# The swapped copy of q: from a VectorE copy to an integer operation in layer 1, and into the DMA transpose in layer 2

## The chip, the core and the metric

The kernel runs on one core of a Trainium2 chip. The number that counts is the device time of one execution in microseconds. The kernel before took 1673.78 us in the median of three runs (1671.57 to 1674.27).

## What is computed

Two layers work on a residual stream of 1024 positions and 1024 channels, each `x <- x + W_out(mixer(RMSNorm(x)) * silu(gate))`, with 16 heads of 64. Layer 1 is causal attention with a forgetting bias, layer 2 is windowed attention in three dilation groups whose results are weighted by their softmax sums.

```python
def fox_mixer(h, w_in, b_f, q_g, k_g):                 # layer 1
    q, k = rms_norm(q, q_g), rms_norm(k, k_g)          # per head, over 64 channels
    c = cumsum(log_sigmoid(f_logit))
    s = einsum('bqhd,bkhd->bhqk', q, k) * scale + c_q - c_k ; causal mask ; softmax ; @ v
def dsw_mixer(h, cos, sin, w_in, q_g, k_g):            # layer 2
    q, k = partial_rotary(rms_norm(q, q_g)), partial_rotary(rms_norm(k, k_g))
    for g, (window, dilation) in enumerate(((128, 1), (512, 4), (2048, 16))):
        o_g, lse_g = dilated_window_attention(q[g], k[g], v[g], window, dilation)
    o = sum_g softmax_g(lse_g) * o_g
```

The inputs and the result are float32.

## The kernel before

**Two halves for each number.** TensorE multiplies float16. To keep float32's precision each operand is split into a high and a low float16 half, and a product is made of three matmuls (high by high, high by low, low by high). The projections (`project`, L688, matmul on L693) stream `xh` and `xl`, each against a slab of weights: 24 matmuls of 384 columns per tile of 128 positions. The columns are those of two heads at once: keys, queries and values.

**From a projection to q and k.** Two tiles of positions make a pair. `heads_tile` (L786) multiplies keys and queries by the gains into `u` (VectorE, L788) and squares them on ScalarE (L793). `heads_sums` sums the squares on VectorE (L806, L808). `heads_pair` (L810) applies the rotation in layer 2 on GpSimd (L820 to L823: `ra`, `rb`, `u`), makes the inverse root (ScalarE L826 to L828, VectorE L829, L830), multiplies `u` by it (VectorE L832), and splits `u` into `hl`: the high half on ScalarE (L834), the low half on GpSimd (L835). `hl` is `[128, 2, 4, 2, 64]`: position, tile of the pair, two keys and two queries, high and low, channel.

**The turn.** `turn` (L837) sends `hl` through one DMA transpose (L840, issued from SyncE's queue SP) of 8 blocks of 128 by 128. In each block of the result `qk_t` the partitions 0 to 63 hold the 64 channels' high half and 64 to 127 the low half of one key or query. A matmul of a query block with a key block contracts over all 128 partitions and gives high by high plus low by low. The two mixed products need the query with its halves exchanged. Before, `qs` holds this: two VectorE copies (L843), each of 64 partitions and 512 float16, move the upper half of the query blocks down and the lower half up. They wait for the transpose to land.

**Scores.** `scores` (L858) takes for each head two matmuls (L863): the first with the query out of `qk_t`, the second with `qs`. The rows of scores go through VectorE (L1110 in layer 1, L1335 in layer 2: bias or mask and the maximum), ScalarE (exponent L1337 or L906, high half of `ph` L1347 or L909), GpSimd (low half L1348 or L912), a second DMA transpose (`ptt<-ph`, L1349 or L913), and the matmuls with the values (L920 to L922). In layer 2 there are 24 rounds of weights with 4 pairs each, 96 pairs; in layer 1 there are 8 rounds, 32 pairs. The scores of a pair are asked for 16 ticks after it (`lsd`), where one tick is two of the eight slabs of a projection.

**What sets the order.** The program is written in one line of time (`Flow`), and `order_engines` (L426) then fixes every engine's order. `plan_engines` (L323) walks through all instructions with a table of durations (`Step.lasts`, L206), of those VectorE operations that keep GpSimd out and are kept out by it (`Step.locks`, L191), and of latest starts worked out from the order on TensorE (`latest_starts`, L304). A copy between two SBUF tiles is such a locking operation in the table, with 60 + 0.45 ns for each column; an operation with a scalar is not, with 110 + 1.04 ns for each. Each engine and the SP queue carry out their instructions in that order, and one that waits holds up all behind it. GpSimd's low half of `ph`, the low half of `hl` and the rotation share one such order. The pools around the change: two buffers of `hl`, six of `qk_t` and `qs` in layer 1, three of each in layer 2.

Of the kernel before, what the change touches and what calls it, by code (L numbers as in the profile page):

```python
# [22 lines left out]
P = 128  # L23
# [5 lines left out]
HD = 64  # L29
# [407 lines left out]
def trunk(ctx, tc, ins, out, cfg):  # L437
    nc = tc.nc
# [7 lines left out]
    def pool(name, bufs, space=None):  # L446
        kw = {} if space is None else dict(space=space)
        return book.pool(ctx.enter_context(tc.tile_pool(name=name, bufs=bufs, **kw)), name, bufs, space)
# [3 lines left out]
    sb = pool("sb", 2)  # L452
# [16 lines left out]
    def lay(shape, dtype, name, tag):  # L469
        return layer["pool"].tile(shape, dtype, name=name, tag=tag, bufs=layer["bufs"][tag])  # L470
# [339 lines left out]
    def heads_pair(gi, t, hd):  # L810

        u, sq, w = hd
        if gi > 0:
            half = ROT // 2
            ti = (gi - 1) * NT + t
            c = cs[:, ti : ti + 2].unsqueeze(2)
            s = sn[:, ti : ti + 2].unsqueeze(2)
            ra = sm.tile([P, 2, 4, ROT], F32, name="ra", tag="ra", bufs=2)
            rb = sm.tile([P, 2, 4, ROT], F32, name="rb", tag="rb", bufs=2)
            nc.gpsimd.tensor_mul(ra, u[:, :, :, :ROT], c.broadcast_to([P, 2, 4, ROT]))  # L820
            nc.gpsimd.tensor_mul(rb[:, :, :, :half], u[:, :, :, half:ROT], s[:, :, :, :half].broadcast_to([P, 2, 4, half]))
            nc.gpsimd.tensor_mul(rb[:, :, :, half:], u[:, :, :, :half], s[:, :, :, half:].broadcast_to([P, 2, 4, half]))
            nc.gpsimd.tensor_add(u[:, :, :, :ROT], ra, rb)  # L823
        v, a, y = w["v"], w["a"], w["y"]
        r = sm.tile([P, 2, 4], F32, name="rs_y", tag="rs_y4")
        nc.scalar.activation(r, v, AF.Ln)  # L826
        nc.scalar.activation(r, r, AF.Exp, scale=-0.5)
        nc.scalar.activation(a, r, AF.Square)  # L828
        nc.vector.scalar_tensor_tensor(a, a, -0.5, v, ALU.mult, ALU.mult)  # L829
        nc.vector.scalar_tensor_tensor(y, a, 1.5, r, ALU.add, ALU.mult)  # L830
        hl = sb.tile([P, 2, 4, 2, HD], F16, name="hl", tag="hl", bufs=cfg["hb"])
        nc.vector.tensor_mul(u, u, y.unsqueeze(3).broadcast_to([P, 2, 4, HD]))  # L832

        nc.scalar.copy(hl[:, :, :, 0], u)  # L834
        nc.gpsimd.tensor_sub(hl[:, :, :, 1], u, hl[:, :, :, 0])  # L835

        def turn():  # L837
            qk_t = lay([P, 8, P], F16, name="qk_t", tag="qk_t")
            qs = lay([P, 2, 2, P], F16, name="qs", tag="qs")
            nc.sync.dma_start_transpose(qk_t, hl.rearrange("p i a b d -> p (i a b d)"))  # L840
            qk = qk_t.rearrange("p (i a) s -> p i a s", i=2)
            for a in (0, HD):
                nc.vector.tensor_copy(qs[a : a + HD], qk[HD - a : P - a, :, 2:4])  # L843
            return qk, qs

        return turn
# [26 lines left out]
    def v_tile(w):  # L873
        vt = lay([P, NT, 2, 129], F16, name="vt", tag="vt")
        nc.scalar.activation(vt[:, :, :, 128], w.sw.unsqueeze(2).broadcast_to([P, NT, 2]), AF.Copy, scale=lim[:, w.layer, 3:4])
        return vt
# [125 lines left out]
    with book.early(nc, cfg["rush"]):  # L1002
        gain_scale(0, gt)
        nb = column_factor(0)
        gain_xt(0)
        split_xt(0, nb)
    with book.early(nc, cfg["rush"] / 2):
        nb = column_factor(1)
# [173 lines left out]
    for hp in range(NHP):  # L1182
# [11 lines left out]
        vt = v_tile(w)  # L1194
        for t in range(NT):
            ps = project(w, tile_cols(0, t))
# [12 lines left out]
            if hp == NHP - 1:  # L1209

                a = max(flow.now + 1, s0 + cfg["due"][t] - 4 * NT + cfg["lpf"] + 9)
# [219 lines left out]
    for ci, (hp, g) in enumerate(order):  # L1431
# [5 lines left out]
        vt = v_tile(w)  # L1437
        qks = [None]
        for t in range(NT):
            if ci == NHP - 1:  # L1440
                reload_x(t)
            ps = project(w, tile_cols(g, nth_tile(g, t)))
# [21 lines left out]
            else:  # L1464
                cmb = {}
# [28 lines left out]
    layer["cm"].__exit__(None, None, None)  # L1494


CFG = dict(out={(False, 0): (), (True, 0): ((18, 20, 22, 24), (0, 0, 1, 1), 3, (4, 6, 8, 10)), (True, 1): ((18, 20, 22, 24), (14, 15, 17, 18), 24, (33, 35, 37, 39))}, take=(((33, 34, 37, 40), 42), ((62, 63, 66, 69), 71)), rush=2000, gate=(((6, 7, 8, 9), (0, 0, 1, 1), 4, (5, 6, 7, 9)), ((44, 45, 46, 47), (26, 28, 30, 32), 36, (38, 40, 42, 44)), ()), bc=((1, 0, 26), (1, 1, 28), (0, 0, 38), (0, 1, 46)), wpool=3, rbufs=8, most=(0, 2), lcm=7, ps=0, pv=100, ph_=100, ph=1, wbufs=8, pl=3, um=3, lpf=8, lsd=((16, 16), (16, 14), (14, 11)), ty2=((0, 4), (1, 5)), hb=2, ub=2, qb=1, nb=3, fox=(((0, 0, 2, 2), (2, 4)), ((0, 0), (4, 4))), due=(29, 33, 39, 45, 35, 41, 49, 57), l1=dict(ga=7, ptt=4, ph=3, p=4, qk_t=6, qs=6, vt=3, gsl=3), l2=dict(ga=4, cmb=4, gsd=4, ptt=3, ph=3, p=2, qk_t=3, qs=3, og=3, vt=3, gsl=3, par=1), wload=(18, 20, 22, 24), wbound=(0, 1, 3, 4), wscale=8, wsplit=(10, 16, 22, 12))


def host_layout(inputs):  # L1500
# [49 lines left out]
```

## Time and profile before

| | |
|---|---|
| three timed runs | 1674.27, 1671.57, 1673.78 us |
| profiled execution | 1674.25 us, its span 1672.1 us |
| granted TensorE clock, mean | 0.996 |
| layer 1's attention | 140 to 560 us of the span |
| layer 2's attention | 620 to 1600 us |
| output projection of layer 2 | from 1600 us |

A group's row names the line, the engine, the operation, what it writes and reads, how often it ran, its busy time, the mean duration in ns, and how long the engine stood idle before it and for what. PE is the matmul part of TensorE, PEld its weight load, DVE is VectorE, ACT ScalarE, POOL GpSimd, SPq the queue that issues the DMAs. A wait's row says who waited for whom, for how long in all, how many times, and the longest. TensorE's busy time counts overlapping matmuls once, and a matmul of 384 columns is shown with 324 ns although the next one begins 163 ns later (192 of them take 31.24 us in the chain of waits); a stall shorter than that overlap doesn't appear as idle.

### The profile page before, as it was taken

Reading aid. Unit: us, or ns where it says so; the run is one execution under the profiler, and the core shown is the slowest. Engines: PE = TensorE matmul, PEld = TensorE weight load, DVE = VectorE, ACT = ScalarE, POOL = GpSimd, SP = SyncE. Lnnn points to the kernel's source line nnn. Section 1 sums busy time; section 2 is a strip of 40 time slices with the busy share of each in tenths; the row PEclk is TensorE's granted clock in tenths of the full one; section 3 lists DMA queues with packets and bytes.
Section 4 is the critical chain, followed back from the end, with each engine's and each line's share of the span. In section 5 each row is a group of like instructions: output and inputs, shape, how many; then the busy total and the mean of one; then the engine's idle time right before and its main releaser. Section 6 shows DMA issues by size and latency. Waiting matters only on the chain.

```text
span 1672.1 us, 37759 instructions
## 1 busy us (share of the span) xinstructions
PE 1615.3 (97%) x13342; PEld 1045.3 (63%) x13342; DVE 1271.4 (76%) x3791; ACT 1067.4 (64%) x2746; POOL 893.2 (53%) x1049
## 2 busy tenths in 40 slices
PE   5999999999989999999999999999999999999999
PEld 3666776766765456666666666666666666666544
DVE  7857888878876597577777797878787888878851
ACT  6656777777766477566666677656665666656630
POOL 4303656666645242155555566667576775857430
PEclk9999999999999999999999999999999999999999
DMA  6344999999999785246665785767657576666852
GB/s 239 114 133 116 204 208 199 211 174 195 213 201 234 218 255 177 88 116 151 144 140 127 164 198 131 174 134 167 134 148 147 129 189 134 150 146 153 191 160 98
DMA packets 597326, 276.07 MB, mean 165 GB/s; under 512 B 444672, under 2 KB 561408, under 8 KB 597136
## 3 DMA queue, kind: packets, MB, share of 16 engines
q1 hardware_dynamic: 597136, 273.67, 69.5%
q8 instruction: 104, 1.70, 0.4%
q14 instruction: 86, 0.70, 0.1%
HBM read 124.35 MB, written 41.22 MB: 99 GB/s over the span
## 4 chain that ended last, share of the span: by engine, by line
PE 56%; DVE 16%; DMA 10%; issue 6%; POOL 5%; ACT 4%; SPq 2%; POOLq 0%; DVEq 0%; ACTq 0%
PE pj L693 41%; PE pj L718 7%; PE s L863 4%; DMA qk_t<-hl 3%; DVE qs L843 3%; DVE w L659 3%; DMA ptt<-ph 2%; DMA raw<-in_w_dsw 1%; POOL ph L1348 1%; POOL hl L835 1%; DVE vm L632 1%; DVE p L1110 1%; DMA yt<-y_d 1%; ACT p L906 1%; DVE u L788 1%
## 5 line engine op out<-in xcount | busy, mean ns | idle before, releaser
L693 PE MATMUL pj<-w,xh 128*128 128x384 f16 (+2 forms) x4864 | 1173.3, 324 | 12.3 <-ACT w L658 4.8
L693 PE MATMUL pj<-w,xl 128*128 128x384 f16 (+2 forms) x2432 | 787.3, 324 | 3.6 <-DVE xl L1265 3.5
L693 PEld LDWEIGHTS <-xh 128*128 128x128 f16 x4864 | 467.9, 98 | 285.8 <-issue 9.3
L693 PEld LDWEIGHTS <-xl 128*128 128x128 f16 x2432 | 238.2, 98 | 159.0 <-issue 5.6
L912 POOL TENSOR_TENSOR ph<-p,ph 128x512 f16<-128x512 f32 (+3 forms) x176 | 172.7, 1001 | 141.2 <-issue 78.8
L1348 POOL TENSOR_TENSOR ph<-p,ph 128x768 f16<-128x768 f32 (+2 forms) x96 | 156.8, 1633 | 112.4 <-ACT ph L1347 100.1
L835 POOL TENSOR_TENSOR hl<-u,hl 128x512 f16<-128x512 f32 x128 | 156.9, 1226 | 82.6 <-ACT hl L834 81.5
L843 DVE COPY qs<-qk_t 64x512 f16<-64x512 f16 x256 | 152.7, 597 | 24.9 <-DMA qk_t<-hl 18.7
L718 PE MATMUL pj<-xh,w 128*128 128x512 f16 x512 | 158.1, 382 | 6.9 <-DVE xr L1487 3.0
L793 ACT ACTIVATE sq<-pj 128x256 f32<-128x256 f32 x256 | 95.7, 377 | 90.4 <-DVE u L788 88.2
L863 PE MATMUL s<-qk_t 128*128 128x128 f16 (+1 forms) x752 | 144.4, 246 | 3.1 <-DMA qk_t<-hl 1.5
L863 PE MATMUL s<-qk_t,qs 128*128 128x128 f16 (+1 forms) x752 | 141.4, 247 | 5.6 <-DVE qs L843 5.2
L659 DVE SCALAR_TENSOR_TENSOR w<-raw,sws,w 128x768 f16<-128x768 f32 x96 | 135.7, 1420 | 4.4 <-ACT w L658 4.3
L788 DVE TENSOR_TENSOR u<-pj,gr 128x256 f32<-128x256 f32 x256 | 106.4, 418 | 36.7 <-PE pj L693 34.8
L906 ACT ACTIVATE p<-p,acc 128x512 f32<-128x512 f32 (+2 forms) x192 | 109.4, 607 | 36.7 <-DVE acc L1110 36.4
L718 PEld LDWEIGHTS <-w 128*128 128x128 f16 x768 | 74.5, 98 | 90.7 <-issue 9.8
L1337 ACT ACTIVATE p<-p,og 128x128 f32<-128x128 f32 (+1 forms) x256 | 104.9, 443 | 28.2 <-DVE og L1335 27.3
L920 PEld LDWEIGHTS <-ptt 128*128 128x128 f16 x1136 | 105.9, 98 | 19.0 <-DMA ptt<-ph 7.6
L630 ACT ACTIVATE jk<-raw 128x768 f16<-128x768 f32 (+2 forms) x88 | 72.2, 820 | 64.2 <-DMA raw<-in_w_dsw 36.6
L834 ACT CAST hl<-u 128x512 f16<-128x512 f32 x128 | 78.8, 616 | 52.4 <-DVE u L832 42.6
L921 PEld LDWEIGHTS <-ptt 128*128 128x128 f16 x1136 | 105.2, 96 | 11.2
L1335 DVE CUSTOM_DVE_ANT_0 p<-s,band 128x256 f32<-128x256 f32 (+1 forms) x256 | 89.7, 373 | 29.0 <-PE s L863 28.8
(212 smaller groups left out, 3003.3 us busy)
## 6 DMA issues: line engine op xcount, KB each, us to landing
raw<-in_w_dsw SPq DMA_DIRECT2D x96, 384.0 KB, 3.9
raw<-in_w_fox SPq DMA_DIRECT2D x32, 384.0 KB, 4.1
og_d<-og SPq DMA_DIRECT2D x64, 132.0 KB, 2.4
cmb<-og_d SPq DMA_DIRECT2D x64, 132.0 KB, 2.7
bc<-c_d SPq DMA_DIRECT2D x32, 256.0 KB, 4.1
gs_d<-ge SPq DMA_DIRECT2D x32, 192.0 KB, 2.1
xt<-in_xt SPq DMA_DIRECT2D x16, 256.0 KB, 5.0
gsf<-gs_d SPq DMA_DIRECT2D x64, 64.0 KB, 2.4
```

What stands on the lines that cost most here:

```text
L659: nc.vector.scalar_tensor_tensor(w[:, 1, :, :n], raw, self.sw, w[:, 0, :, :n], ALU.mult, ALU.subtract)
L693: nc.tensor.matmul(ps[:, :n], a[:, k, cols], w.slab(k, j), start=(k == 0 and i == 0), stop=(k == KT - 1 and i == 2))
L718: nc.tensor.matmul(ps[m], ws[h].slab(k, j)[:, m * P : (m + 1) * P], a[:, k, 512 * b : 512 * (b + 1)], start=(k == 0 and x == 0), stop=(k = ...
L788: nc.vector.tensor_mul(u[:, t % 2].rearrange("p (a b) d -> p a b d", a=2), ps[:, : 4 * HD].rearrange("p (a b d) -> p a b d", a=2, b=2), gr ...
L835: nc.gpsimd.tensor_sub(hl[:, :, :, 1], u, hl[:, :, :, 0])
L843: nc.vector.tensor_copy(qs[a : a + HD], qk[HD - a : P - a, :, 2:4])
L863: nc.tensor.matmul(s[:, c0 : c0 + cnt * P].rearrange("p (c s) -> p c s", c=cnt), q, kk[:, j : j + cnt, e], start=(h == 0), stop=(h == 1 an ...
L906: nc.scalar.activation(p, p, AF.Exp, bias=acc, scale=-1.0)
L912: (nc.gpsimd if pool_l else nc.vector).tensor_sub(ph[:, e, 1, cols], p, ph[:, e, 0, cols])
L920: nc.tensor.matmul(o[:, e, :], hi, vt[:, j, e, HD:], start=(b == 0), stop=False, skip_group_check=True)
L921: nc.tensor.matmul(o[:, e, :HD], hi, vt[:, j, e, :HD], start=False, stop=False, skip_group_check=True)
L1348: nc.gpsimd.tensor_sub(ph[:, 1], st["p"], ph[:, 0])
```

## The change

In layer 1 (`gi` is 0) the two operations that make `qs` stay in their place, after the transpose. Their views are read as 32-bit integers, 256 columns in place of 512, and the copy becomes a bitwise OR with zero.

In layer 2 `qs` is gone. `hl` has 6 rows in place of 4 for each tile: a VectorE copy writes the queries a second time, with high and low exchanged, after GpSimd has made the low half. The transpose then has 12 blocks in place of 8, and the swapped query is `qk[:, :, 4:]`. So the copy is one of 128 partitions and 512 float16 for each pair in place of two of 64 partitions, and stands ahead of the transpose, not behind it.

```diff
-        hl = sb.tile([P, 2, 4, 2, HD], F16, name="hl", tag="hl", bufs=cfg["hb"])
+        nb = 6 if gi else 4
+        hl = sb.tile([P, 2, nb, 2, HD], F16, name="hl", tag="hl", bufs=cfg["hb"])
         nc.vector.tensor_mul(u, u, y.unsqueeze(3).broadcast_to([P, 2, 4, HD]))
 
-        nc.scalar.copy(hl[:, :, :, 0], u)
-        nc.gpsimd.tensor_sub(hl[:, :, :, 1], u, hl[:, :, :, 0])
+        nc.scalar.copy(hl[:, :, :4, 0], u)
+        nc.gpsimd.tensor_sub(hl[:, :, :4, 1], u, hl[:, :, :4, 0])
+        if gi:
+            nc.vector.tensor_copy(hl[:, :, 4:], hl[:, :, 2:4, ::-1])
 
         def turn():
-            qk_t = lay([P, 8, P], F16, name="qk_t", tag="qk_t")
-            qs = lay([P, 2, 2, P], F16, name="qs", tag="qs")
+            qk_t = lay([P, 2 * nb, P], F16, name="qk_t", tag="qk_t")
             nc.sync.dma_start_transpose(qk_t, hl.rearrange("p i a b d -> p (i a b d)"))
             qk = qk_t.rearrange("p (i a) s -> p i a s", i=2)
+            if gi:
+                return qk, qk[:, :, 4:]
+            qs = lay([P, 2, 2, P], F16, name="qs", tag="qs")
             for a in (0, HD):
-                nc.vector.tensor_copy(qs[a : a + HD], qk[HD - a : P - a, :, 2:4])
+                dst, src = (v.bitcast(I32) for v in (qs[a : a + HD], qk[HD - a : P - a, :, 2:4]))
+                nc.vector.tensor_single_scalar(dst, src, 0, ALU.bitwise_or)
             return qk, qs
```

The table of buffers loses `qs=3` in layer 2. Since the planner takes durations and locks by kind of operation, the order on every engine is made anew. On TensorE it is nearly the same. The two places below belong to the 63rd pair of layer 2, in the profile before at 1278 to 1290 us.

VectorE before, from the inverse root of the next pair to the sum of outputs; `qs<-qk_t` are the two copies, `vt` the values' low half, `u<-pj` the first product of the next tile:

```order
L829 SCALAR_TENSOR_TENSOR pj<-pj,rs_v 128x8
L830 SCALAR_TENSOR_TENSOR pj<-pj,rs_y 128x8
L788 TENSOR_TENSOR u<-pj,gr 128x256
L832 TENSOR_TENSOR u<-u,pj 128x512
L843 COPY qs<-qk_t 64x512
L799 SCALAR_TENSOR_TENSOR vt<-pj,vt 128x2x64
L843 COPY qs<-qk_t 64x512
L1387 TENSOR_TENSOR ob<-ob,cmb 128x260
```

VectorE in the change, the 63rd pair's own second product of `u` and the copy into `hl`:

```order
L830 SCALAR_TENSOR_TENSOR pj<-pj,rs_y 128x8
L1375 TENSOR_REDUCE mm<-cmb 128x4
L833 TENSOR_TENSOR u<-u,pj 128x512
L788 TENSOR_TENSOR u<-pj,gr 128x256
L838 COPY hl<-hl 128x2x256
L799 SCALAR_TENSOR_TENSOR vt<-pj,vt 128x2x64
```

The copy now stands two rows behind the product from which ScalarE and GpSimd still have to make `hl`, and the next tile's work stands behind it.

GpSimd before, at the same pair (`ph` is a low half of the exponents, `hl` that of keys and queries, `ra` and `rb` the rotation of the next pair, `cmb` the weighting of the groups):

```order
L1376 TENSOR_TENSOR wt<-mm,cmb 128x8
L1348 TENSOR_TENSOR ph<-p,ph 128x768
L835 TENSOR_TENSOR hl<-u,hl 128x8x64
L820 TENSOR_TENSOR ra<-u,cs 128x128
L821 TENSOR_TENSOR rb<-u,sn 128x8x8
```

GpSimd in the change:

```order
L1382 TENSOR_TENSOR wt<-mm,cmb 128x8
L836 TENSOR_TENSOR hl<-u,hl 128x2x4x64
L1354 TENSOR_TENSOR ph<-p,ph 128x768
L1385 TENSOR_TENSOR cmb<-cmb,wt 128x8x65
L820 TENSOR_TENSOR ra<-u,cs 128x128
```

Here `hl` has moved ahead of `ph`, so that a long GpSimd operation follows it at once; elsewhere in layer 2 mostly `ra` follows, as before.

More of the change, by code (lines that the diff above doesn't have):

```diff
@@ L1494, in trunk @@
     layer["cm"].__exit__(None, None, None)
-CFG = dict(out={(False, 0): (), (True, 0): ((18, 20, 22, 24), (0, 0, 1, 1), 3, (4, 6, 8, 10)), (True, 1): ((18, 20, 22, 24), (14, 15, 17, 18), 24, (33, 35, 37, 39))}, take=(((33, 34, 37, 40), 42), ((62, 63, 66, 69), 71)), rush=2000, gate=(((6, 7, 8, 9), (0, 0, 1, 1), 4, (5, 6, 7, 9)), ((44, 45, 46, 47), (26, 28, 30, 32), 36, (38, 40, 42, 44)), ()), bc=((1, 0, 26), (1, 1, 28), (0, 0, 38), (0, 1, 46)), wpool=3, rbufs=8, most=(0, 2), lcm=7, ps=0, pv=100, ph_=100, ph=1, wbufs=8, pl=3, um=3, lpf=8, lsd=((16, 16), (16, 14), (14, 11)), ty2=((0, 4), (1, 5)), hb=2, ub=2, qb=1, nb=3, fox=(((0, 0, 2, 2), (2, 4)), ((0, 0), (4, 4))), due=(29, 33, 39, 45, 35, 41, 49, 57), l1=dict(ga=7, ptt=4, ph=3, p=4, qk_t=6, qs=6, vt=3, gsl=3), l2=dict(ga=4, cmb=4, gsd=4, ptt=3, ph=3, p=2, qk_t=3, qs=3, og=3, vt=3, gsl=3, par=1), wload=(18, 20, 22, 24), wbound=(0, 1, 3, 4), wscale=8, wsplit=(10, 16, 22, 12))
+CFG = dict(out={(False, 0): (), (True, 0): ((18, 20, 22, 24), (0, 0, 1, 1), 3, (4, 6, 8, 10)), (True, 1): ((18, 20, 22, 24), (14, 15, 17, 18), 24, (33, 35, 37, 39))}, take=(((33, 34, 37, 40), 42), ((62, 63, 66, 69), 71)), rush=2000, gate=(((6, 7, 8, 9), (0, 0, 1, 1), 4, (5, 6, 7, 9)), ((44, 45, 46, 47), (26, 28, 30, 32), 36, (38, 40, 42, 44)), ()), bc=((1, 0, 26), (1, 1, 28), (0, 0, 38), (0, 1, 46)), wpool=3, rbufs=8, most=(0, 2), lcm=7, ps=0, pv=100, ph_=100, ph=1, wbufs=8, pl=3, um=3, lpf=8, lsd=((16, 16), (16, 14), (14, 11)), ty2=((0, 4), (1, 5)), hb=2, ub=2, qb=1, nb=3, fox=(((0, 0, 2, 2), (2, 4)), ((0, 0), (4, 4))), due=(29, 33, 39, 45, 35, 41, 49, 57), l1=dict(ga=7, ptt=4, ph=3, p=4, qk_t=6, qs=6, vt=3, gsl=3), l2=dict(ga=4, cmb=4, gsd=4, ptt=3, ph=3, p=2, qk_t=3, og=3, vt=3, gsl=3, par=1), wload=(18, 20, 22, 24), wbound=(0, 1, 3, 4), wscale=8, wsplit=(10, 16, 22, 12))
 def host_layout(inputs):
```

## The prediction

> **What bounds the kernel now.** I read the busy shares first, then a table by stage, then who waited for whom on TensorE. The page's first part and the chain of waits by line:
>
> ```profile
> PE 1615.3 (97%) x13342; PEld 1045.3 (63%) x13342; DVE 1271.4 (76%) x3791; ACT 1067.4 (64%) x2746; POOL 893.2 (53%) x1049
> PE pj L693 41%; PE pj L718 7%; PE s L863 4%; DMA qk_t<-hl 3%; DVE qs L843 3%; DVE w L659 3%; DMA ptt<-ph 2%; DMA raw<-in_w_dsw 1%; POOL ph L1348 1%; POOL hl L835 1%; DVE vm L632 1%; DVE p L1110 1%; DMA yt<-y_d 1%; ACT p L906 1%; DVE u L788 1%
> ```
>
> TensorE works for 97% of the span. The chain gives 3% to the copies on L843, 50 us, but that is no gain to be had: a chain runs through buffers and orders while TensorE keeps working beside it. What the change can return is TensorE's idle time where it waits for q.
>
> The attention of layer 1 and of layer 2 as two stretches (TensorE, weight load, VectorE, ScalarE, GpSimd, clock, DMA share), then the instructions that touch `qs` alone (TensorE, weight load, VectorE):
>
> ```profile
> 140.00:560.00 420.00, 404.69 (x4156) 280.95 (x4155) 324.56 (x1035) 306.56 (x738) 236.49 (x230) 0.99 0.94 201
> 620.00:1600.00 980.00, 966.11 (x7812) 626.80 (x7811) 778.82 (x2359) 633.63 (x1749) 590.67 (x761) 1.00 0.65 150
> ...
> 140.00:560.00 420.00, 71.14 (x320) 31.28 (x320) 36.32 (x64) 0.99 0.94 201
> 620.00:1600.00 980.00, 70.26 (x432) 40.89 (x432) 116.39 (x192) 1.00 0.65 150
> ```
>
> In layer 2 TensorE idles 980 - 966.1 = 13.9 us. VectorE is at 79% there, 15% of that in the copies. Waits of TensorE and of its weight load, layer 2 ahead of the second line of dots, layer 1 behind it (total, times, longest):
>
> ```profile
> PE s L863 <- DVE qs L843: 4.0, 5, 1.6
> PE s L863 <- DMA qk_t<-hl: 1.5, 3, 0.9
> PE pj L693 <- DVE peak L897: 1.2, 3, 0.8
> PE pj L693 <- DVE u L832: 0.8, 4, 0.2
> PE pj L693 <- DVE vt L799: 0.7, 2, 0.4
> ...
> PEld L863 <- DVE qs L843: 6.3, 9, 1.8
> PEld L863 <- DMA qk_t<-hl: 2.4, 4, 1.0
> ...
> PE s L863 <- DVE qs L843: 1.2, 2, 0.9
> PEld L863 <- DVE qs L843: 2.5, 3, 1.3
> ```
>
> For q, layer 2 loses between 4.0 + 1.5 = 5.5 us (idle matmul part) and 6.3 + 2.4 = 8.7 us (idle weight load, which also sees waits that the end of the last matmul covers). I take 7, in 9 + 4 = 13 waits. Layer 1 loses 1.2 to 2.5.
>
> **One late pair, step by step.** The 63rd pair of layer 2, the rows of each engine in turn:
>
> ```profile
> 1280.24 1.16 POOL L835 TENSOR_TENSOR hl<-u,hl 128x512 f16<-128x512 f32 x1
> 1281.36 0.46 POOL L820 TENSOR_TENSOR ra<-u,cs 128x128 f32<-128x128 f32 x1
> ...
> 1286.44 1.16 POOL L835 TENSOR_TENSOR hl<-u,hl 128x512 f16<-128x512 f32 x1
> ...
> 1282.17 1.24 SPq L840 DMA_TRANSPOSE qk_t<-hl  x1
> ...
> 1286.72 1.02 DVE L843 COPY qs<-qk_t 64x512 f16<-64x512 f16 x1 [2.11 <-DMA qk_t<-hl]
> 1287.76 0.29 DVE L799 SCALAR_TENSOR_TENSOR vt<-pj,vt 128x128 f16<-128x128 f32 x1
> 1288.06 0.74 DVE L843 COPY qs<-qk_t 64x512 f16<-64x512 f16 x1
> ...
> 1286.75 0.34 PE L863 MATMUL s<-qk_t 128*128 128x128 f16 x2 [0.27 <-DMA qk_t<-hl]
> 1288.86 0.23 PE L863 MATMUL s<-qk_t,qs 128*128 128x128 f16 x1 [1.57 <-DVE qs L843]
> ```
>
> GpSimd ends `hl` at 1281.40, the transpose is issued at 1282.17 and lands near 1286.7. The first score matmul starts; the second needs both copies, which end at 1288.80. They take 1.02 and 0.74 us, and the first overlaps GpSimd's operation from 1286.44 to 1287.60. So the copies are 2.1 us of the way behind the landing, and TensorE idles 0.27 + 1.57.
>
> **Prices.** The copy's durations (min, median, max in ns) in layer 2 and in layer 1, and operations of its kind: integers with a constant, float32 with a constant, and two inputs, most of 128 or 192 columns:
>
> ```profile
> L843 DVE COPY qs<-qk_t x192: 285/290/2198, 717.1 to 1590.5; 64x512 f16<-64x512 f16 x192
> ...
> L843 DVE COPY qs<-qk_t x64: 286/394/1278, 140.5 to 511.9; 64x512 f16<-64x512 f16 x64
> ...
> L1297 DVE TENSOR_SCALAR par_i<-par_i x1: 217/217/217, 645.7 to 645.7; 128x128 int32<-128x128 int32 x1
> ...
> L1046 DVE TENSOR_SCALAR zt<-zt x1: 220/220/220, 87.8 to 87.8; 128x128 f32<-128x128 f32 x1
> L1047 DVE TENSOR_TENSOR zt<-zt,fa x1: 279/279/279, 88.3 to 88.3; 128x128 f32<-128x128 f32 x1
> ...
> L545 DVE TENSOR_SCALAR rt<-rt_pf x8: 177/183/1268, 564.4 to 566.1; 128x24 f32<-128x24 f32 x8
> L555 DVE TENSOR_SCALAR rt<-rt x5: 252/260/261, 567.3 to 576.1; 128x192 f32<-128x192 f32 x5
> L557 DVE TENSOR_TENSOR rt<-rt x5: 357/358/359, 568.0 to 576.7; 128x192 f32<-128x192 f32 x5
> ```
>
> Undisturbed, a copy takes 285 ns; its mean in layer 2 is 116.39 / 192 = 606 ns, so 0.32 us of holding on average, up to 1.9.
>
> *Layer 1's integer operation.* With a constant, 128 columns take 217 to 220 ns and 192 take 260, so (260 - 220) / 64 = 0.63 ns a column, and 256 columns come to 260 + 64 x 0.63 = 300 ns. On the slower line of two inputs, (358 - 279) / 64 = 1.23, they come to 437. The one integer row lies on the fast line, so I take 300, the copy's own time. Whether GpSimd still holds it up no row shows; float32 with a constant meets a hold (1268 against a median of 183 on L545), and being as fast, I take it that integers do. Layer 1 then changes by 0 us, with bounds of -2.5 (its waits for `qs` gone) and +2.5 (as many again).
>
> *Layer 2's removal and addition.* 192 copies of 606 ns go; 96 copies of 512 columns come, at 0.29 us plus the holding. For the holding I have two rows: the 0.32 us of today's copies, and GpSimd's mean operation of 590.67 / 761 = 0.78 us at a load of 590.67 / 980 = 60%, hence 0.47 if the copy, woken by GpSimd's own end of `hl`, finds the next one started and waits it out. I take 0.4, so a copy of 0.7 us. It lies on the way to the scores, between `hl` and the transpose.
>
> *The longer transpose.* The same queue already sends 8 and 12 blocks for the probabilities: three of 512 columns from 1096 us, four of 768 from 1062 us. Issue in ns, then landing in us:
>
> ```profile
> L1349 SPq DMA_TRANSPOSE ptt<-ph x3: 1232/1232/1232, 1096.3 to 1112.7; - x3
> DMA to landing us min/median/max: 2.7/2.7/4.3
> ...
> L1349 SPq DMA_TRANSPOSE ptt<-ph x4: 1401/1420/2235, 1062.9 to 1089.6; - x4
> DMA to landing us min/median/max: 3.2/3.4/4.0
> ```
>
> The undisturbed landing grows from 2.7 to 3.2, 0.5 us for each of 96 transposes. That is 48 us more of the 16 DMA engines in 980, the share going from 0.65 to about 0.70. The issue takes 0.19 us more of SP, 18 us in all, hidden unless SP has fallen behind.
>
> **The sum.** On the way of a late pair go two copies and what stands between and ahead of them: 2 x 0.606 = 1.21 us by the mean, 2.1 in the pair above. There come 0.7 + 0.5 = 1.2. So a late pair gains between 0 and 0.9 us. With 0.4 for each of the 13 waits, of which many are shorter than that, I count 3 of the 7 us as gone: **-3.0** (bounds -7 and, where the copy meets a long `ph` on GpSimd, +8, below). VectorE's load in layer 2 falls by 116.4 - 96 x 0.7 = 49 us, from 79% to 74%; TensorE's other waits for VectorE there (`peak`, `u`, `vt` and four smaller) are about 5 us, of which I take a fifth: **-1.0** (bounds -5 and 0). Busier DMA engines and SP: **+0.5** (0 to +2). Layer 1: **0**. In all -3.5. Against the profiled execution's 1674.25 us (a span of 1672.1 and 2.15 around it) that is 1670.75; it lies 0.47 above the median of the runs shown, so the median goes from 1673.8 to **1670.3**. The cover under all of this is TensorE's own work: a pair's scores come some 16 us behind its projection, and 83 of 96 pairs don't make it wait today. If every pair became 1 us later than I think, only those 13 and a few beside them would show it.
>
> **Rivals.**
>
> *A late copy (slower).* The copy wakes when GpSimd ends `hl`, and GpSimd's next instruction is ready at that instant, as `ra` 1281.36 behind `hl` above. Where the new order puts `ph` there, it holds the copy for a whole long operation:
>
> ```profile
> L1348 POOL TENSOR_TENSOR ph<-p,ph 128x768 f16<-128x768 f32 x40 | 66.3, 1658 | 56.6 <-ACT ph L1347 56.6
> ```
>
> Then the copy takes 0.29 + 1.66 = 1.95, and the way changes by 1.95 + 0.5 - 1.21 = +1.2 us. SP stands at the transpose meanwhile, with the next loads and the probabilities' transposes behind it. The row orders have `ph` behind `hl` in 14 of 96 pairs; if those delays reach half of the 13 waits, that is +8, less the 1 from a freer VectorE: **1681**. It decides when the added holding is over 0.9 us at the late pairs. For it: the maximum of 2198 ns. Against: GpSimd mostly goes on with `ra`, 0.46 us. [...]
>
> *Nearly all waits go.* The freer VectorE makes `u` and the maxima earlier, so late pairs aren't late: -7 and -2 beside it, **1665**. For it: the pair above was late because its copies met other work. Against: the landing took 4.5 us there, which VectorE doesn't change.
>
> *The integer operation is free of GpSimd.* It would take 300 ns in place of a mean 36.32 / 64 = 567, 17 us of VectorE in layer 1, and end its 2.5 us of waits: 1670.3 - 2.5 = **1668**. Against: TensorE idles little for it. [...]
>
> *The change does nothing.* Landing and copy give back what the copies took: **1673.8**.
>
> **How the numbers follow.** About 0.2%, 3.3 us, is what this kernel's runs can tell from no change. The forecast of -3.5 has 0.48 and lies on that line: 0.25 faster, 0.23 same. Nearly all waits go: 0.14, faster. The free integer operation: 0.06 (0.04 faster, 0.02 same). Nothing: 0.10, same. The late copy: 0.22 (0.21 slower, 0.01 same). That makes 0.43 faster, 0.36 same, 0.21 slower. The forecast's own range is 1667 to 1674. The whole range, 1663 to 1681, takes in the bounds on the good side and half of the late copy; less than 2 in 10 lie outside.
>
> **What would show it.** Right: L838 with 96 copies of about 0.7 us and VectorE near 74% in layer 2; transposes of 12 blocks landing in 3.2 us or more; TensorE's waits for `qk_t` in layer 2 near 4 us with none for `qs`; L849 near 300 ns at best, with a median and a maximum as before. Wrong: a minimum under 250 ns on L849 or a maximum under 400; copies of 1.5 us; waits for `qk_t` over 9 us; idle time of TensorE in layer 2 above 14 us; or a gain or loss in the stretch from 430 to 620 us, of which I have said nothing and which the new order also touches.

## The result and the profile after

The changed kernel takes 1663.99 us (median of four runs, 1662.55 to 1665.39) beside 1674.03 us (1671.57 to 1677.13) for the kernel before on the same chip: a ratio of 0.9945, 95% interval 0.9929 to 0.9961. That is 10 us less by the medians and 9 by the ratio. The forecast was 1670.3, in a range of 1663 to 1681 that holds the time, by 1 us at its lower end; the forecast's own range of 1667 to 1674 does not. The sign is right, but the gain is nearly three times the 3.5 us forecast and lands on the price given for the rival "nearly all waits go" (1665). The profiled execution took 1665.39 us with a span of 1663.6, against 1674.25 and 1672.1 before.

Where in the program the time went is read from the rows of the transposes of layer 2, whose first and last start stand behind the durations (min, median, max in ns). Before:

```profile
L840 SPq DMA_TRANSPOSE qk_t<-hl x96: 1231/1240/4789, 713.9 to 1584.6; - x96
```

After, with the time from issue to landing:

```profile
L842 SPq DMA_TRANSPOSE qk_t<-hl x96: 1384/1461/4393, 713.7 to 1577.3; - x96
DMA to landing us min/median/max: 3.2/3.7/7.1
```

The first transpose starts 0.2 us earlier and the last 7.3 us earlier. So in these two profiled executions nothing was gained in layer 1 and up to 714 us; about 7.1 of the 8.5 us of the span were gained over the 96 pairs of layer 2, and the last 1.2 behind them.

The busy shares of the engines on the profile's page after:

```profile
PE 1612.1 (97%) x13342; PEld 1045.5 (63%) x13342; DVE 1198.8 (72%) x3695; ACT 1063.0 (64%) x2746; POOL 893.5 (54%) x1049
```

The chain of waits after can be followed back only to 439 us (the shares on its page add up to 73%), so the chains of the two pages don't compare as a whole. Both cover 620 to 1600 us: there TensorE's projections (L693) are 50.0% of the stretch before and 72.8% after, and the 3.7% of the copies on L843 are gone. The two stretches of the attention in the kernel after, layer 1 and layer 2 (TensorE, weight load, VectorE, ScalarE, GpSimd, clock, DMA share):

```profile
140.00:560.00 420.00, 405.38 (x4168) 282.12 (x4167) 326.89 (x1033) 306.09 (x737) 241.23 (x230) 1.00 0.93 201
620.00:1600.00 980.00, 971.00 (x7864) 629.88 (x7862) 704.58 (x2267) 630.74 (x1751) 587.02 (x761) 1.00 0.71 165
```

TensorE idles 980 - 971.0 = 9.0 us in layer 2, against 13.9. That is 4.9 us of a gain of some 7. Over the whole span the idle time fell by 5.3 of 8.5 us, and the other 3.2 are busy time, 1615.3 to 1612.1 for the same 13342 matmuls. Those may be stalls shorter than the 0.16 us by which two matmuls overlap (324 ns shown, the next one after 163), which count as busy; no row shows them one by one. VectorE's load in the stretch fell by 74 us, from 778.8 to 704.6, where 49 were forecast; 72 of these are the copies. Layer 1 is as it was (404.7 busy and 405.4). Who waited for whom in layer 2 of the kernel after (total, times, longest): TensorE, behind the first dots its weight load, behind the second VectorE:

```profile
PE s L869 <- DMA qk_t<-hl: 4.2, 4, 1.5
PE pj L693 <- DVE xl L1271: 1.0, 1, 1.0
PE pj L718 <- DVE xr L1493: 1.0, 1, 1.0
PE pj L693 <- DVE peak L903: 0.9, 2, 0.7
PE pj L693 <- DVE u L833: 0.9, 6, 0.2
...
PEld L869 <- DMA qk_t<-hl: 6.4, 6, 1.9
...
DVE hl L838 <- POOL hl L836: 49.8, 38, 2.3
```

The scores no longer wait for `qs`, but they wait longer for the landing: 4.2 us in place of 5.5 for both, and 6.4 in place of 8.7 at the weight load. By these rows the scores' waits shrank by 1.3 to 2.3 us, far less than the time did. VectorE stands idle for `hl` ahead of the new copies for 49.8 us in 38 waits, more than the 44.2 us that they take.

The durations (min, median, max in ns) of the copy of layer 2:

```profile
L838 DVE COPY hl<-hl x96: 280/295/1726, 713.3 to 1577.0; 128x512 f16<-128x512 f16 x96
```

And of the integer operation of layer 1:

```profile
L849 DVE TENSOR_SCALAR qs<-qk_t x64: 286/346/1274, 140.0 to 511.9; 64x256 int32<-64x256 int32 x64
```

The integer operation takes 286 ns undisturbed, as the copy of 512 float16 columns did (286), and its maximum stays (1274 beside 1278). 33 of the 64 take over 330 ns, and in the trace each of these overlaps a GpSimd operation that began ahead of it; the longest, at 388.62 us, ends 0.15 us behind the `ph` beside it. So GpSimd holds it up like the copy.

### The profile page after: what moved, and what is told of

It is laid out like the page before. It is cut to its first block, busy times and chain, and to the rows that moved or that the text cites. A ratio compares the mean times of both kernels' runs of the same rounds, so it can differ in the third digit from the quotient of the medians.

```text
span 1663.6 us, 37721 instructions
## 1 busy us (share of the span) xinstructions
PE 1612.1 (97%) x13342; PEld 1045.5 (63%) x13342; DVE 1198.8 (72%) x3695; ACT 1063.0 (64%) x2746; POOL 893.5 (54%) x1049
## 4 chain that ended last, share of the span: by engine, by line
PE 57%; DVE 6%; DMA 4%; issue 2%; ACT 2%; SPq 1%; POOL 1%; DVEq 0%; ACTq 0%; POOLq 0%
PE pj L693 44%; PE pj L718 7%; PE s L869 4%; DMA qk_t<-hl 2%; DVE w L659 1%; PE ob L928 1%; PE ob L926 1%; PE ob L927 1%; DVE xs L1266 1%; DMA ptt<-ph 1%; POOL ph L918 1%; DMA xn_d<-xg 1%; DMA yt<-y_d 1%; ACT w L658 1%; SPq L919 0%
## 5 line engine op out<-in xcount | busy, mean ns | idle before, releaser
L693 PE MATMUL pj<-w,xh 128*128 128x384 f16 (+2 forms) x4864 | 1174.2, 324 | 11.4 <-ACT w L658 4.8
L693 PE MATMUL pj<-w,xl 128*128 128x384 f16 (+2 forms) x2432 | 788.5, 324 | 4.2 <-DVE xl L1271 4.2
L693 PEld LDWEIGHTS <-xh 128*128 128x128 f16 x4864 | 467.3, 98 | 285.1 <-issue 10.6
L693 PEld LDWEIGHTS <-xl 128*128 128x128 f16 x2432 | 238.4, 98 | 160.1 <-issue 6.3
L1354 POOL TENSOR_TENSOR ph<-p,ph 128x768 f16<-128x768 f32 (+2 forms) x96 | 161.5, 1682 | 138.4 <-ACT ph L1353 131.0
L836 POOL TENSOR_TENSOR hl<-u,hl 128x512 f16<-128x512 f32 x128 | 150.9, 1179 | 71.5 <-ACT hl L835 59.1
L718 PE MATMUL pj<-xh,w 128*128 128x512 f16 x512 | 157.4, 379 | 7.5 <-DVE xr L1232 3.5
L869 PE MATMUL s<-qk_t 128*128 128x128 f16 (+1 forms) x1184 | 151.1, 242 | 4.7 <-DMA qk_t<-hl 4.2
L718 PEld LDWEIGHTS <-w 128*128 128x128 f16 x768 | 74.0, 98 | 89.1 <-issue 8.9
L926 PEld LDWEIGHTS <-ptt 128*128 128x128 f16 x1136 | 106.1, 98 | 16.5 <-DMA ptt<-ph 5.2
L927 PEld LDWEIGHTS <-ptt 128*128 128x128 f16 x1136 | 105.6, 97 | 11.4 <-issue 0.2
L928 PEld LDWEIGHTS <-ptt 128*128 128x128 f16 x1136 | 105.7, 97 | 0.0
L820 POOL TENSOR_TENSOR ra<-u,cs 128x128 f32<-128x128 f32 x96 | 44.5, 463 | 108.5 <-DVE u L788 98.4
```

The lines of the kernel that those rows point to most:

```text
L693: nc.tensor.matmul(ps[:, :n], a[:, k, cols], w.slab(k, j), start=(k == 0 and i == 0), stop=(k == KT - 1 and i == 2))
L718: nc.tensor.matmul(ps[m], ws[h].slab(k, j)[:, m * P : (m + 1) * P], a[:, k, 512 * b : 512 * (b + 1)], start=(k == 0 and x == 0), stop=(k = ...
L836: nc.gpsimd.tensor_sub(hl[:, :, :4, 1], u, hl[:, :, :4, 0])
L869: nc.tensor.matmul(s[:, c0 : c0 + cnt * P].rearrange("p (c s) -> p c s", c=cnt), q, kk[:, j : j + cnt, e], start=(h == 0), stop=(h == 1 an ...
L926: nc.tensor.matmul(o[:, e, :], hi, vt[:, j, e, HD:], start=(b == 0), stop=False, skip_group_check=True)
L927: nc.tensor.matmul(o[:, e, :HD], hi, vt[:, j, e, :HD], start=False, stop=False, skip_group_check=True)
```

## The experiments

The expectations name the theories by letters. **A**: the way from a pair's transpose to its scores got shorter, so late scores are less late. **B**: VectorE's load in layer 2 fell, and every microsecond of it costs some time (B1); or only the standing of VectorE at a landing that is late, as the 2.11 us of the 63rd pair before (B2). **C**: the integer operation in layer 1. **D**: the new order of the instructions by itself. One thousandth of the ratio is 1.67 us. Each kernel was timed in five rounds against the kernel before on the same chip.

### Which part of the change gains

Layer 1's part alone (edit of the kernel before):

```
-                nc.vector.tensor_copy(qs[a : a + HD], qk[HD - a : P - a, :, 2:4])
+                if gi:
+                    nc.vector.tensor_copy(qs[a : a + HD], qk[HD - a : P - a, :, 2:4])
+                    continue
+                dst, src = (v.bitcast(I32) for v in (qs[a : a + HD], qk[HD - a : P - a, :, 2:4]))
+                nc.vector.tensor_single_scalar(dst, src, 0, ALU.bitwise_or)
```

> The integer operation in layer 1 alone; layer 2 keeps its two copies behind the transpose. The change gained 10 us (1674.0 to 1664.0). Theory A (the gain is layer 2's shorter way from the transpose to the scores): 1673 to 1675, since TensorE waits only 1.2 to 2.5 us for these operations in layer 1. Theory B (the gain is VectorE's lower load in layer 2): the same, 1673 to 1675. Theory C (the integer operation is free of GpSimd and brings a good part): 1668 to 1671, with a maximum of the operation under 400 ns. Theory D (the new order alone brings it): anywhere from 1668 to 1677, with the operation's durations as before.

Measured: 1672.13 us, ratio 0.9986 [0.9975, 0.9997], or -2.3 us.

Layer 2's part alone (edit of the changed kernel):

```
-                dst, src = (v.bitcast(I32) for v in (qs[a : a + HD], qk[HD - a : P - a, :, 2:4]))
-                nc.vector.tensor_single_scalar(dst, src, 0, ALU.bitwise_or)
+                nc.vector.tensor_copy(qs[a : a + HD], qk[HD - a : P - a, :, 2:4])
```

> Layer 2 as in the change (a third pair of rows in the transpose), layer 1 with its two float16 copies as before. A and B: 1663 to 1666, all of the gain. C: 1667 to 1670. D: anything up to 1672.

Measured: 1665.33 us, 0.9942 [0.9924, 0.9960], or -9.7 us. This is the whole change's gain: layer 2 alone makes it, and on top of it layer 1's operation adds nothing that can be measured, which leaves no room for C. What it gains alone, -2.3, barely stands clear of zero, and since its durations are those of the copy, the likely source, if the gain is real, is another order of the instructions.

The changed kernel once more, in a later comparison:

> The changed kernel as it is, beside the next three on one chip: 1663 to 1666.

Measured: 1663.11 us, 0.9951 [0.9937, 0.9966].

### What the exchange costs in all

Edit of the changed kernel: no copy into `hl`, eight blocks, and the second matmul of the scores takes the query as it is. The products of high and low halves are left out; TensorE does the same number of matmuls.

```
-            nc.vector.tensor_copy(hl[:, :, 4:], hl[:, :, 2:4, ::-1])
...
-                return qk, qk[:, :, 4:]
+                return qk, qk[:, :, 2:4]
```

> Layer 2 leaves the exchange of halves out: no copies at all, the transpose has 8 blocks, and the second score matmul takes the same query as the first (so the products of high and low halves are left out of layer 2's scores). Layer 1 with the integer operation. This is the ceiling. A: the waits for q in layer 2 go almost wholly, another 3 to 5 us below the change, 1659 to 1661. B: VectorE has 50 us less to do than in the change, 1660 to 1662, with about as much gained outside the score matmuls. If neither the longer transpose nor the added copy costs anything any more: 1664, as the change.

Measured: 1661.51 us, 0.9915 [0.9896, 0.9934], or -14.2 us. Layer 2 as a stretch in this kernel (columns as above):

```profile
620.00:1600.00 980.00, 972.93 (x7876) 631.89 (x7875) 668.24 (x2177) 633.14 (x1756) 593.58 (x761) 1.00 0.65 153
```

And the one wait of its scores there:

```profile
PE s L866 <- DMA qk_t<-hl: 1.6, 2, 1.4
```

So the exchange of layer 2 cost some 14 us before, by this kernel, whose order is also new, and the change saves 9 to 10 of these. The waits of the kernel before show only about half of that: the scores' 5.5 to 8.7 us. An account of layer 2 that starts from "what does TensorE wait for q" starts from too small a sum.

### Whether VectorE's time is what costs

The changed kernel, with the two old copies put back behind each transpose of layer 2, into a buffer that nobody reads. The scores don't wait for them.

```
             if gi:
+                qd = sb.tile([P, 2, 2, P], F16, name="qd", tag="n2k", bufs=cfg["nb"])
+                with book.early(nc, 16000):
+                    for a in (0, HD):
+                        nc.vector.tensor_copy(qd[a : a + HD], qk[HD - a : P - a, :, 2:4])
                 return qk, qk[:, :, 4:]
```

> The change, and beside it in layer 2 the two old copies of 64 partitions behind each transpose, into a buffer that nobody reads: VectorE's load is as before or higher (about 820 us of 980), but no score waits for these copies. A: 1664 to 1667, TensorE's waits for qk_t stay near 4 to 6 us. B: 1669 to 1673, most of the gain is lost again, through u, peak and the values' halves.

Measured: 1682.08 us, 1.0050 [1.0030, 1.0070]. That is 18 us over the changed kernel, slower than the kernel before, and 9 us above the range that B had. In the edit `book.early` moves the planned latest start of the copies forward by 16 us, because the planner gives an operation that nobody reads 30 us of time. Layer 2 of this kernel as a stretch, and behind the dots the copies themselves:

```profile
620.00:1600.00 980.00, 962.36 (x7780) 625.10 (x7779) 811.93 (x2436) 630.95 (x1745) 589.95 (x756) 1.00 0.70 161
...
L848 DVE COPY qd<-qk_t 64x512 f16<-64x512 f16 x192 | 130.4, 679 | 20.4 <-DMA qk_t<-hl 16.1
```

The waits there, of TensorE and behind the dots of VectorE:

```profile
PE pj L693 <- DVE vt L799: 7.1, 7, 1.7
PE pj L693 <- DVE u L833: 4.2, 3, 2.3
PE s L873 <- DMA qk_t<-hl: 3.1, 3, 1.9
...
DVE vt L799 <- ACT vt L798: 35.0, 40, 2.8
DVE hl L838 <- POOL hl L836: 19.0, 23, 1.7
DVE qd L848 <- DMA qk_t<-hl: 16.1, 21, 1.8
```

Scores wait no more than in the changed kernel (3.1 against 4.2 us), yet the projections now wait for `vt` (7.1 against 0.3) and `u` (4.2 against 0.9), which VectorE carries out behind the copies. So VectorE's work at the turn, or its standing at the landing (B2), costs time though no score waits for it, which A alone doesn't allow; 18 us is also well over the 5 us that another order cost by itself (below). What the shorter way to the scores gave, this run doesn't show. The 18 us are 0.16 for each of the 107 us by which the load of the stretch rose (811.9 against 704.6), or 0.14 for each of the 130 us of the copies themselves.

The copy of the change made a second time, into an unread buffer, behind the first:

```
             nc.vector.tensor_copy(hl[:, :, 4:], hl[:, :, 2:4, ::-1])
+            qd = sb.tile([P, 2, 2, P], F16, name="qd", tag="n2k", bufs=cfg["nb"])
+            with book.early(nc, 16000):
+                nc.vector.tensor_copy(qd.rearrange("p i a (b d) -> p i a b d", b=2), hl[:, :, 2:4, ::-1])
```

> The change, with the copy into the third pair of rows made a second time in layer 2, into a buffer that nobody reads. It adds some 40 us to VectorE's load in layer 2 (705 to about 747 of 980) and, unlike the two copies behind the landing, no wait for a DMA. Theory B1 (load counts): the two copies behind the landing added 107 us of load and 16 to 18 us of time, so 0.16 us for each us, and this one 40 x 0.16 = 6: 1669 to 1672. Theory B2 (not the load but VectorE's waiting in order for the landing, 16 us of idle time there, is what cost): 1664 to 1666. Theory A (only the way to the scores counts): 1664 to 1666.

Measured: 1667.38 us, 0.9977 [0.9963, 0.9991]. Layer 2 as a stretch, and behind the dots the second copy:

```profile
620.00:1600.00 980.00, 969.33 (x7826) 627.75 (x7825) 730.49 (x2355) 630.91 (x1746) 597.42 (x760) 1.00 0.72 164
...
L841 DVE COPY qd<-hl 128x512 f16<-128x512 f16 x96 | 39.1, 407 | 0.0
```

The second copies, 39 us of their own and 26 us more load on VectorE, with no landing to stand at, cost (0.9977 - 0.9951) x 1673 = 4.3 us: 0.11 of the copies' time or 0.17 of the load (GpSimd is busy 10 us longer as well). This speaks against B2 alone, but weakly. The two intervals overlap a little (0.9963 to 0.9991 and 0.9937 to 0.9966). And in the profiled execution the score matmuls of layer 2 run over 868.0 us (713.7 to 1581.7) where the changed kernel's run over 866.6 (718.2 to 1584.8), only 1.4 longer, while 3.8 us are lost between the last score and the end of the span (82.6 and 78.8).

### Whether any microsecond of VectorE costs

Three tests put or take VectorE time elsewhere, in the preparation of the next round's weights. First, in the kernel before, one of the two maxima of each round goes to ScalarE, by a setting:

```
-most=(0, 2)
+most=(0,)
```

> The kernel before, nothing of q changed; one of the two maxima of each round of weights (VectorE, 0.94 us) becomes a sum of squares on ScalarE (0.82 us). In layer 2 VectorE loses 24 x 0.94 = 23 us of 779. B1: by 10 us of time for 74 us of load, 3 us faster: 1670 to 1672. B2 and A: no change, 1673 to 1675. If ScalarE is as tight as VectorE: slower than 1675.

Measured: 1672.39 us, 1.0006 [0.9992, 1.0019]. VectorE's load fell by 12 us, not by 23 (762.2 in place of 774.5 between 620 and 1595 us), ScalarE's rose by 13, and the time stayed. (The profiled execution took 1665.2 us, 7 below the median, so these rows are those of a faster one.) That leaves open whether ScalarE gave back what VectorE saved. So, in the kernel before, the maxima over a third of the columns, with nothing put elsewhere (in both layers the rest of each block is left out of the bound):

```
-                nc.vector.tensor_reduce(self.vm[:, i : i + 1], raw, AX.XY, ALU.max, apply_absolute_value=True)
+                nc.vector.tensor_reduce(self.vm[:, i : i + 1], raw[:, :, :128], AX.XY, ALU.max, apply_absolute_value=True)
```

> The kernel before, with each of VectorE's maxima over a raw block of weights (line 632) taken over a third of its columns: the rest of the block is left out of the bound, nothing else changes. In 620 to 1595 us VectorE should lose about 54 times 0.6 = 33 us, nearly as much as the change takes from it net (72 us) but in another place: not in the chain of a round's pair. If any VectorE microsecond of layer 2 costs 0.13 to 0.16 us of time (theory B): -4 to -5 us, 1668 to 1669 beside a before of 1673. If only work in the pair's own chain costs time (the reading that moving the maxima to ScalarE suggests): 0 to -1. If there ScalarE's addition had cancelled VectorE's relief: again -4 to -5.

Measured: 1675.08 us, 1.0011 [0.9997, 1.0024]. Layer 2 as a stretch, and behind the dots what TensorE waited for there:

```profile
620.00:1600.00 980.00, 964.81 (x7804) 626.00 (x7803) 756.45 (x2359) 631.11 (x1745) 586.46 (x759) 1.00 0.65 149
...
PE s L863 <- DVE qs L843: 5.5, 10, 1.2
PE pj L693 <- DVE u L832: 2.2, 7, 1.0
```

22 us less of VectorE (756.5 against 778.8, with 409 ns for a maximum in place of 932) gave nothing that the time shows; 0.16 for each would have been -3.6, outside the interval of -0.5 to +4.0 us. TensorE's waits for `qs` and `u` are not smaller. The opposite test, in the changed kernel: a second, unread maximum over half the columns.

```
                 nc.vector.tensor_reduce(self.vm[:, i : i + 1], raw, AX.XY, ALU.max, apply_absolute_value=True)
+                if self.layer:
+                    vx = sm.tile([P, 1], F32, name="vx", tag="vx")
+                    nc.vector.tensor_reduce(vx, raw[:, :, : self.n // 2], AX.XY, ALU.max, apply_absolute_value=True)
```

> The changed kernel with a second, unread maximum of VectorE over half the columns of each of its raw blocks of weights in layer 2 (a new line behind line 632). In 620 to 1595 us that is some 54 maxima of about 0.53 us, 28 us in all by the 0.409 us of a 256-column one and the 0.943 us of a 768-column one: as much as the copy made twice put on VectorE, which cost 4.3 us beside the changed kernel, but here in the preparation of the next weights and not between a pair's projection and its scores. If any microsecond on VectorE costs the same (B): +4.3, about 1667.5. If only work in the pair's chain costs time: 0 to +1, 1663 to 1665.

Measured: 1666.54 us, 0.9957 [0.9942, 0.9972], so 1.0 to 2.0 us over the two comparisons of the changed kernel (0.9951 and 0.9945). Layer 2 as a stretch:

```profile
620.00:1600.00 980.00, 968.02 (x7824) 627.88 (x7822) 725.75 (x2317) 627.90 (x1745) 587.15 (x760) 1.00 0.71 162
```

21 us more in this place cost 1 to 2 us, where the load theory has 3.5; the intervals are too wide to tell these two apart by this run alone. Whether the price of a microsecond depends on its place is not shown by these runs. In the profiled execution with the second maximum the score matmuls of layer 2 run over 871.4 us (716.4 to 1587.8), longer than with the copy made twice. And every edit gives the engines a new order. Counted in the traces by operation and tile, at least 255 of VectorE's 3791 instructions must move to turn the order of the kernel before into that with the smaller maxima; beside the changed kernel it is 347 of 3695 for the copy made twice, 473 for the two old copies and 46 for the second maximum. A new order alone can cost some 5 us (shown below), more than the 3.6 us that the smaller maxima were to return.

### Whether other engines can carry it

The changed kernel, with the exchanged rows written from `u` by ScalarE and GpSimd, and no VectorE copy in layer 2:

```
-            nc.vector.tensor_copy(hl[:, :, 4:], hl[:, :, 2:4, ::-1])
+            uq = u[:, :, 2:4]
+            nc.scalar.copy(hl[:, :, 4:, 1], uq)
+            nc.gpsimd.tensor_sub(hl[:, :, 4:, 0], uq, hl[:, :, 4:, 1])
```

> The change, but the third pair of rows is written by ScalarE (high half, out of u, about 0.4 us) and GpSimd (low half, about 0.7 us); VectorE has no copy at all in layer 2 (about 663 us of load, as with the exchange left out). B1: 42 us less of load, as in the kernel without the exchange, 1661 to 1663, unless GpSimd (587 to about 654 us of 980) becomes late, then 1664 to 1668. A: GpSimd's second low half lies on the way in the place of the copy, so 1663 to 1666.

Measured: 1670.01 us, 0.9989 [0.9976, 1.0001]. Layer 2 as a stretch, and behind the dots the durations of the added subtraction:

```profile
620.00:1600.00 980.00, 967.90 (x7837) 627.01 (x7836) 662.21 (x2166) 658.83 (x1842) 659.52 (x856) 1.00 0.72 164
...
L840 POOL TENSOR_TENSOR hl<-u,hl x96: 662/671/1387, 709.5 to 1575.7; 128x256 f16<-128x256 f32 x96
```

VectorE has 42 us less than in the changed kernel, GpSimd 72 us and ScalarE 28 us more, and most of the gain is lost, which no theory had. The subtraction of 671 ns replaces a copy of 295 in the same place of the pair. So VectorE's total alone doesn't set the time. That it is the work between a pair's projection and its scores, on whichever engine, fits this run but isn't shown by it: the profiled execution took 1666.0 us, 4 below the median, and here too the order is new.

### The late landings that are left

Four to six transposes of layer 2 in the changed kernel still land too late. The 61st pair of the kernel after in the timeline, the rows of GpSimd, VectorE, SP and TensorE in turn (start, duration, and in brackets the wait):

```profile
1258.44 1.16 POOL L836 TENSOR_TENSOR hl<-u,hl 128x512 f16<-128x512 f32 x1
...
1258.72 1.69 DVE L659 SCALAR_TENSOR_TENSOR w<-raw,sws,w 128x768 f16<-128x768 f32 x1
1260.34 0.28 DVE L838 COPY hl<-hl 128x512 f16<-128x512 f16 x1
...
1257.77 1.14 SPq L1418 DMA_DIRECT2D cmb<-og_d  x2
1258.96 1.08 SPq L1422 DMA_DIRECT2D gsd<-gs_d  x1
1260.09 0.93 SPq L620 DMA_DIRECT2D raw<-in_w_dsw  x2
1261.12 2.32 SPq L842 DMA_TRANSPOSE qk_t<-hl  x1
...
1268.28 0.83 PE L869 MATMUL s<-qk_t 128*128 128x128 f16 x8 [1.45 <-DMA qk_t<-hl]
```

`hl` is ready at 1259.60; the copy stands behind a scaling of weights until 1260.34, and the transpose behind loads of raw weights until 1261.12; it lands 7.1 us later, beside these loads. Edit of the changed kernel: the raw weights of layer 2 are loaded later.

```
-wload=(18, 20, 22, 24)
+wload=(22, 24, 26, 28)
```

> The changed kernel with the loads of raw weights of layer 2 put behind the pair's transpose on SyncE's queue (due at steps 22, 24, 26, 28 in place of 18, 20, 22, 24), so that the first transposes of the last group's rounds, which landed after 5.7 to 7.1 us behind these loads, land in about 3.7. If the rest of the exchange's price is this late landing (theory A): the waits of scores for qk_t in 620 to 1590 us fall from 4.2 and 6.4 to under 2, and the time by 1 to 3 us, to 1660.5 to 1662.5 beside 1663.5. If it is load (theory B): 1663 to 1664. If the weights now come late: waits of the projection for the weights' scaling, and 1666 or more.

Measured: 1666.38 us, 0.9949 [0.9931, 0.9968]: no gain. What TensorE and its weight load waited for in layer 2 of this kernel:

```profile
PE pj L718 <- DVE xr L1493: 2.1, 1, 2.1
...
PE s L869 <- DMA qk_t<-hl: 0.3, 1, 0.3
...
PEld L718 <- issue: 4.4, 9, 2.2
...
PEld L869 <- DMA qk_t<-hl: 0.6, 1, 0.6
```

The waits went as A said, from 4.2 to 0.3 and from 6.4 to 0.6, but the time of the whole kernel did not follow. The score matmuls of layer 2 in the changed kernel, and behind the dots in this one (the times are the first and last start):

```profile
L869 PE MATMUL s<-qk_t x864: 216/219/273, 718.2 to 1584.8; 128*128 128x128 f16 x122, 128*128 128x256 f16 x51
...
L869 PE MATMUL s<-qk_t x864: 216/219/273, 720.3 to 1581.9; 128*128 128x128 f16 x122, 128*128 128x256 f16 x51
```

They run over 861.6 us in place of 866.6. So in the profiled execution the pairs gained 5.0 us, about as much as the waits lost (3.9 to 5.8), and 3.4 of it went again between the last score and the end (82.2 in place of 78.8). There the output projection (L718) waits for VectorE's `xr` (2.1 in place of 1.0), and its weight load for nothing that the profile shows (4.4 in place of 1.1). What a wait for q is worth can't be fixed more closely from this: layer 2's part alone, whose layer 2 is that of the change, has its scores over 870.2 us (714.6 to 1584.8), 3.6 more than the change, though only the order differs there.

### The order by itself

The kernel before with the integer operation in both layers; the exchange does not go by DMA, and the undisturbed durations are the copies' own:

```
-                nc.vector.tensor_copy(qs[a : a + HD], qk[HD - a : P - a, :, 2:4])
+                dst, src = (v.bitcast(I32) for v in (qs[a : a + HD], qk[HD - a : P - a, :, 2:4]))
+                nc.vector.tensor_single_scalar(dst, src, 0, ALU.bitwise_or)
```

> The kernel before with the integer operation in place of the two copies in both layers; no exchange by DMA. VectorE's load does not change (286 ns before and after for one piece). If the integer operation only changes the order of issue (theory D): within 2 us of before, 1671 to 1675, and so the gain of the change is none of the order's. If a shorter operation in the pair's chain is worth what the load theory says (B): 96 times two copies of 0.37 us by one integer operation of 0.35 us for the same bytes is 0. If the integer operation stays free of GpSimd's hold in layer 2: about -3.

Measured: 1678.60 us, 1.0030 [1.0015, 1.0046], so 5 us slower, which no theory had. The operation's group in layer 2, and behind the dots a wait of TensorE there:

```profile
L844 DVE TENSOR_SCALAR qs<-qk_t 64x256 int32<-64x256 int32 x192 | 120.0, 625 | 22.9 <-DMA qk_t<-hl 17.9
...
PE pj L693 <- DVE u L832: 4.6, 6, 0.8
```

In layer 2 the operation takes 625 ns in the mean, the copy 606: the same. What differs is the plan, whose table has the copy keep GpSimd out and the integer operation not, so the instructions stand in another order (at least 563 of VectorE's 3791 have moved); TensorE waits 4.6 us for `u` in place of 0.8. The profiled execution of this kernel took 1673.7 us, below its median, so its rows can't account for the whole 5 us. With the durations as they were, the other order is the only difference left. So a new order can cost some 5 us, and the parts of the change's gain can't be told apart to better than that. D as the source of the gain is still unlikely: three different orders that share the exchange by DMA (the change, layer 2 alone, later loads) all gain 8 to 10 us.

## Why the prediction was right, and where it was not

**The sign and the range** held, the range by 1 us, which is partly luck: most of the gain did not lie in the term that the forecast put first. Nor is the lower end of 1663 what the bounds come to: -7, -5, 0 and -2.5 add up to 1659.3. What held is that layer 2's copies cost time and that the DMA transpose carries the exchange for less.

**The scores' waits (-3.0).** Measured -1.3 at the matmuls and -2.3 at the weight load, so somewhat less than forecast. The run with later loads takes away nearly all the waits that are left; in its trace the pairs gain by it and the end of the layer loses, and the time stays.

**VectorE's relief (-1.0, bounds -5 and 0).** This is the term that was mis-sized. I took a fifth of the 5 us that TensorE visibly waits for VectorE elsewhere. Without the scores' 1.3 to 2.3 us, 6 to 9 of the measured 8 to 10 us are left, where this term and the next had -0.5 together. The runs give another price: unread copies at the turn cost 0.11 and 0.14 of their own time (39 and 130 us of copies), and the kernel without the exchange, with 116 us of copies fewer, was 14 us faster, 0.12 of them. By that price the 72 us by which the copies shrank (116.4 to 44.2) come to 8 to 10 us. VectorE's work is thus enough to account for the gain; since each of these runs also has a new order, they don't show that it is the whole cause. The step behind it that failed is the premise that what the change can return is TensorE's idle time where it waits for q: idle time in layer 2 fell by 4.9 us, of which the waits for q are 1.3, and some 7 us were gained there.

**The copy in layer 2 (0.7 us).** Measured 44.22 / 96 = 0.46 in the mean, with a median of 295 ns. I had put its holding at 0.4 us, and it was 0.17; so 72 us of copies went from VectorE, not 49, and its share of layer 2 is 72%, not 74%.

**The transposes (+0.5 for busier DMA and SP).** The undisturbed landing of 12 blocks is 3.2 us as forecast, the median rose from 3.4 to 3.7, the issue's from 1.24 to 1.46 us, and the DMA share from 0.65 to 0.71 (0.70 was forecast). What that term is worth in time no run here shows alone.

**Layer 1 (0).** The operation takes 286 ns (300 forecast) and GpSimd holds it up as before (1274 ns at most, in place of 1278); the whole change does no better than layer 2's part. Read as 32-bit integers the same float16 data gain nothing: 286 ns undisturbed for both.

**The late copy (1681).** It happened, in half of the pairs for which it was named, and no score waited for it. In the trace after, `ph` stands behind `hl` in 14 of 96 pairs. In seven of them `hl` is followed by `ph` at once, and these have the seven longest copies, 1714 to 1726 ns, near the 1.95 us of the rival. The 63rd pair:

```profile
1274.72 1.65 POOL L1354 TENSOR_TENSOR ph<-p,ph 128x768 f16<-128x768 f32 x1
1274.80 1.72 DVE L838 COPY hl<-hl 128x512 f16<-128x512 f16 x1 [2.30 <-POOL hl L836]
```

In the other seven `ph` begins 2.6 us behind `hl`, and the copy takes 280 ns. The transposes for which TensorE's weight load waits in layer 2 belong to six other pairs (37, 61, 69, 77, 85 and 93). In the 63rd pair `ph` starts 0.08 us ahead of the copy, and the copy ends 0.15 us behind `ph`. And 39 of the 96 copies take over 330 ns; in the trace each of these 39 overlaps a GpSimd operation that began ahead of it.

**Nearly all waits go (1665).** The time was this rival's, its mechanism half at most. A freer VectorE fits the runs, as it said; but the waits did not all go (6 for `qk_t` at the weight load are left, of 13 for either), and in the run where nearly all went the time stayed.

**The order in front of layer 2.** I had named the stretch of 430 to 620 us as one of which I had said nothing; layer 2's first transpose starts within 0.2 us of where it did, so in the profiled executions it gave and took nothing.

What stays open: how the 8 to 10 us divide between VectorE's work, the shorter way to the scores and the new order, which the runs fix to some 5 us only; and through which of the instructions behind the copies (`u`, `vt`, the maxima of the scores) VectorE's work costs most.

## What to carry to other kernels

Where the bounding engine is 97% busy, its visible waits for an operand need not be the whole price of making that operand. Here they were 5.5 to 8.7 us, and the kernel that leaves the making out was 14 us faster. An unread copy in the same place tests whether such work costs time although nobody waits for it; here it did (130 us of unread copies cost 18 us in one run, 39 us cost 4.3 in another). Where a planner sets the order from a table of costs, take such a price as rough: with the durations unchanged a new order moved the time by some 0.3%, so that a small gain of one edit is to be confirmed in a second order.

## What was not expected of the hardware

A bitwise operation of VectorE with a constant takes the same 286 ns for 256 columns of int32 as a copy for 512 columns of float16 on 64 partitions, and the copy between tiles on 128 partitions takes 280 at best. The bitwise operation is as fast as the copy that it replaces, and GpSimd's operations hold it up as long (1274 ns at most, in place of 1278). A DMA transpose of 12 blocks in place of 8 takes 0.5 us more to land undisturbed (3.2 and 2.7), but only 0.3 in the median (3.7 and 3.4). What the extra traffic cost in time no run here shows alone.
